# Reusing loaded weights in the state-space matmuls, joining the sample matmuls to the prompt matmuls, and claiming slots before the work

## The chip, the cores and the metric

One Trainium2 chip, all eight cores, two dies of four (cores 0 to 3 and 4 to 7). Each core runs the same program on its own prompt row and 16 sample rows. The metric is the device time in microseconds of the slowest core. Time before: 3663.6 us, median of 3 runs (3660.78 to 3669.47).

Some executions fall into a slow state, in which one die, sometimes both, has a lower granted TensorE clock and the run takes longer: 12 of the 39 executions of the kernel before in the rounds of the experiments took 3763.6 to 4310.9 us, with 0.81 to 0.95 on the slower die. Only fast runs (3657.7 to 3670.2 us for this kernel, clock 0.98 on all cores) are compared here. In the profile lines PE is TensorE, the matmul engine, and PEld its weight loads; DVE is VectorE, ACT ScalarE, POOL GpSimd and SP SyncE; L669 is line 669 of the kernel. Because the slowest of eight cores is a noisy number, I also give the *mean core*: the mean span of all cores of those dies whose mean granted clock was over 0.98, over all timed runs of the rounds named. For the kernel before it is 3654.6 us (80 cores, standard deviation 4.8 us).

## The reference, cut to what matters

Four layers. Each has a large input projection, a gated convolution, a state-space branch, a merge, an output projection and a feed-forward part. The change is in the state-space branch:

```python
bu = einsum('blgc,gpc->blgp', u, bbar)             # gather: input into the 64 complex states of each group
h  = associative_scan(a, bu)                       # state_t = Abar * state_{t-1} + Bbar u_t
y  = einsum('blgp,gcp->blgc', h, c) + d * u        # read the state out
ys = gelu(y); ys = ys * sigmoid(ys @ w_glu + b)
```

A prompt of 2048 positions is processed in two halves of 1024. The 16 sample rows, one step each, ride along with the first half.

## The kernel before: the parts that the change touches

The Python program records operations; a list scheduler with assumed costs then fixes one static order for each engine and assigns buffer slots. A tile takes its slot when the first operation that names it is scheduled. An operation is scheduled only if all its slots are there:

```python
def feasible(o, t):
    need = {}
    for tl in o.tiles:
        if tl.slot is None:
            need.setdefault(tl.pool, []).append(tl)
    for p, tls in need.items():
        if len(p.free) < len(tls):
            return False
        ...                                    # and a reserve for the tiles that come first in the program
```

One state-space pass (`ssm_f`, 4 a layer and half, so 32 in all) as PE sees it, cut. Every `e.matmul` makes two instructions, a weight load and a matmul (23912 of each on the page). The tilings are those that the kernel asks for and the profile prints: "array tiled 128x64" stands for matmuls with weights of 128 rows by 64 columns, placed at column 0 or 64 (two column groups; `128*64` at L1033), "64x128" for weights of 64 rows, placed at row 0 or 64 (two row groups; `64*128` at L1107), "full array" for weights of 128 by 128 (`128*128`):

```python
# gather: 32 matmuls of 64 columns, array tiled 128x64
gg[...]  += Wv(h)[:, q, g2, ri, :] . uv(h)[:, q, g2, :]          # S.pe(subs, [(gg,)], (128, 64))
if hs:                                                            # first half: 16 sample matmuls of 16 columns
    gsb[...] = Wv(0)[:, q, g2, ri, :] . us()[:, q, g2, :]         # its own S.pe, its own weight loads
...                                                               # DVE: rotate, scan, rotate back -> vt
# direct part of the output: 8 matmuls of 128 and 8 of 64 columns, full array
yb[g2] += KTv(0)[:, q, g2, :] . uvb()[:, :, q, g2, :]
yb[g2] += KTv(1)[:, q, g2, :] . uv(0)[:, q, g2, :]
if hs:                                                            # 24 sample matmuls of 16 columns, own S.pe
    ysb += KTv(0)[:, q, g2, :] . us()[:, q, g2, :]
    ysb += CDv(0)[:, q, ri, :] . AS0Z[:, g2, ri, 4 * f + q, :]    # ri = 0, 1
# state part of the output: 64 matmuls of 64 columns, array tiled 64x128, row groups g2 in turn
for q, h:
    for i, (o, ri, kk) in enumerate(((0, 0, 0), (256, 1, 0), (512, 1, 1), (768, 0, 1))):
        for g2 in range(2):
            yb[g2] += CDv(h)[64*g2:64*g2+64, q, ri, :] . vt[64*g2:64*g2+64, o+q*64:...]
```

The scheduler makes PE wait for its last operation where the tiling of the array changes (`o.forced = lastpe`).

## Time and profile before

| | before |
|---|---|
| median | 3663.6 us |
| PE busy | 96% |
| weight loads, matmuls | 23912, 23912 |
| start to start, projection matmul of 512 / 384 / 272 columns | 216 / 162 / 116 ns |
| start to start beyond the columns' own time, whole core | 237 us |

These lines are from the page of the kernel before: busy time, granted clock in 40 slices, the queue that brings instructions (packets, MB, share), the chain that ended last by engine, and the costliest groups (count, then busy us and mean ns, then idle time ahead of them).

```profile
span 3663.7 us, 67385 instructions; the slowest of 8 cores (3647.5 to 3663.7 us)
PE 3504.0 (96%) x23912; PEld 1979.7 (54%) x23912; DVE 1618.6 (44%) x2889; ACT 1141.7 (31%) x2151; POOL 608.7 (17%) x799
...
PEclk9799999999999999999999999999999999999999
...
q8 instruction: 202, 3.31, 0.4%
...
PE 88%; DVE 4%; issue 3%; DMA 3%; ACT 1%; SPq 1%; DVEq 0%; ACTq 0%; POOL 0%; POOLq 0%
...
L669 PE MATMUL ps<-H,RING 128*128 128x512 bf16 (+2 forms) x12160 | 2194.9, 340 | 23.5 <-DVE H L726 9.7
L669 PEld LDWEIGHTS ps<-H,RING 128*128 128x128 bf16 x12160 | 1191.5, 99 | 965.9 <-issue 52.3
```

PE is the bottleneck, and its projection matmuls (starts 216, 162 or 116 ns apart) hide their 99 ns loads. What a new order can win is 237 us in which PE stands still. The columns' own time in that figure is an estimate; at 216 ns for 512 columns the trace gives 238 us again (excesses of over 10 ns, slowest core).

### The profile page before, as it was taken

Reading aid. Unit: us, or ns where it says so; the run is one execution under the profiler, and the core shown is the slowest. Engines: PE = TensorE matmul, PEld = TensorE weight load, DVE = VectorE, ACT = ScalarE, POOL = GpSimd, SP = SyncE. Lnnn points to the kernel's source line nnn. Section 1 sums busy time; section 2 is a strip of 40 time slices with the busy share of each in tenths; the row PEclk is TensorE's granted clock in tenths of the full one; section 3 lists DMA queues with packets and bytes.
Section 4 is the critical chain, followed back from the end, with each engine's and each line's share of the span. In section 5 each row is a group of like instructions: output and inputs, shape, how many; then the busy total and the mean of one; then the engine's idle time right before and its main releaser. Section 6 shows DMA issues by size and latency. Waiting matters only on the chain.

```text
span 3663.7 us, 67385 instructions; the slowest of 8 cores (3647.5 to 3663.7 us)
## 1 busy us (share of the span) xinstructions
PE 3504.0 (96%) x23912; PEld 1979.7 (54%) x23912; DVE 1618.6 (44%) x2889; ACT 1141.7 (31%) x2151; POOL 608.7 (17%) x799
## 2 busy tenths in 40 slices
PE   6699999999999999999999899999999999999998
PEld 3466666666666666666664344444444444444443
DVE  8745555465454654543244331354224442254313
ACT  4443234332353322533134320243103421042202
POOL 4232210322103221030000200002000110002000
PEclk9799999999999999999999999999999999999999
DMA  7444557435574355854338544574445644474443
GB/s 157 115 82 70 114 139 149 87 66 113 138 155 86 62 113 135 185 110 84 70 71 196 116 77 71 98 169 74 75 77 115 144 70 81 70 146 79 79 72 87
DMA packets 252804, 384.14 MB, mean 105 GB/s; under 512 B 157632, under 2 KB 180800, under 8 KB 246848
## 3 DMA queue, kind: packets, MB, share of 16 engines
q0 software_dynamic: 67968, 243.30, 39.5%
q1 hardware_dynamic: 184512, 136.53, 12.8%
q8 instruction: 202, 3.31, 0.4%
q14 instruction: 122, 1.00, 0.1%
HBM read 567.06 MB, written 56.12 MB: 170 GB/s over the span
## 4 chain that ended last, share of the span: by engine, by line
PE 88%; DVE 4%; issue 3%; DMA 3%; ACT 1%; SPq 1%; DVEq 0%; ACTq 0%; POOL 0%; POOLq 0%
PE ps L669 83%; DMA yT<-X 1%; PE ps L702 1%; PE ps L1107 1%; DVE SC L561 1%; DVE H L726 1%; PE ps L1033 1%; PE ps L908 1%; PE ps L1080 0%; DVE X L1246 0%; DMA scv<-CIN 0%; SPq L632 0%; PE ps L895 0%; DMA X<-xsT 0%; DVE R L1225 0%
## 5 line engine op out<-in xcount | busy, mean ns | idle before, releaser
L669 PE MATMUL ps<-H,RING 128*128 128x512 bf16 (+2 forms) x12160 | 2194.9, 340 | 23.5 <-DVE H L726 9.7
L669 PEld LDWEIGHTS ps<-H,RING 128*128 128x128 bf16 x12160 | 1191.5, 99 | 965.9 <-issue 52.3
L669 PE MATMUL ps<-R,RING 128*128 128x384 bf16 (+2 forms) x6400 | 1162.1, 339 | 19.7 <-DMA R<-dy 11.4
L669 PEld LDWEIGHTS ps<-R,RING 128*128 128x128 bf16 x6400 | 624.2, 98 | 517.8 <-issue 35.4
L656 POOL DMA_DIRECT2D RING<-wpk x472 | 253.0, 537 | 2635.0 <-PE ps L669 2431.7
L1268 DVE TENSOR_TENSOR R<-SC,ps 128x384 bf16<-128x384 f32 (+2 forms) x440 | 255.8, 583 | 786.7 <-PE ps L669 773.6
L1267 ACT ACTIVATE SC<-ps 128x384 f32<-128x384 f32 (+2 forms) x440 | 226.1, 515 | 1208.0 <-PE ps L669 1199.6
L1246 DVE TENSOR_TENSOR X<-X,ps 128x384 f32<-128x384 f32 (+2 forms) x480 | 269.8, 582 | 448.2 <-PE ps L669 445.2
L700 ACT ACTIVATE H<-X 128x384 bf16<-128x384 f32 (+2 forms) x304 | 156.6, 539 | 198.4 <-DVE X L1246 178.7
L726 DVE SCALAR_TENSOR_TENSOR H<-X,PRM,SC 128x384 bf16<-128x384 f32 (+2 forms) x304 | 183.0, 672 | 35.0 <-ACT SC L707 34.8
L1240 POOL TENSOR_TENSOR R<-TB,SC 128x384 bf16<-128x384 f32 (+1 forms) x160 | 168.1, 1063 | 113.1 <-DVE SC L1237 101.4
L1237 DVE TENSOR_TENSOR SC<-SC,ps 128x384 f32<-128x384 f32 (+1 forms) x160 | 92.7, 584 | 163.5 <-PE ps L669 78.6
L1236 ACT ACTIVATE SC<-ps 128x384 f32<-128x384 f32 (+1 forms) x160 | 81.4, 515 | 248.2 <-PE ps L669 219.8
L1213 DVE TENSOR_TENSOR TB<-TB,ps 128x384 f32<-128x384 f32 (+2 forms) x160 | 89.9, 582 | 128.6 <-PE ps L669 124.6
L1172 DVE TENSOR_TENSOR CIN<-ps,SC 128x384 f32<-128x384 f32 (+2 forms) x80 | 47.0, 587 | 200.7 <-ACT SC L1171 192.6
L561 DVE TENSOR_TENSOR SC<-TB 128x512 f32<-128x512 f32 (+1 forms) x160 | 124.1, 785 | 8.1 <-PE ps L908 0.6
L1158 ACT ACTIVATE TB<-ps 128x384 f32<-128x384 f32 (+1 forms) x160 | 78.9, 516 | 85.8 <-PE ps L669 85.4
L702 PE MATMUL ps<-H,ONESB 128*128 128x384 bf16 (+2 forms) x320 | 78.1, 348 | 27.5 <-ACT H L700 26.8
L561 POOL TENSOR_TENSOR TB<-TB 128x512 f32<-128x512 f32 (+1 forms) x72 | 89.3, 1242 | 42.3 <-DVE R L835 20.7
L1225 DVE TENSOR_TENSOR R<-R,SC 128x384 bf16<-128x384 bf16 (+2 forms) x80 | 46.4, 588 | 88.8 <-ACT SC L1223 86.7
L899 ACT ACTIVATE TAB<-ps 128x512 bf16<-128x512 f32 x60 | 35.5, 597 | 133.0 <-PE ps L895 132.8
L1171 ACT ACTIVATE SC<-ps 128x384 f32<-128x384 f32 (+2 forms) x80 | 41.0, 513 | 95.7 <-PE ps L669 95.5
(180 smaller groups left out, 1633.1 us busy)
## 6 DMA issues: line engine op xcount, KB each, us to landing
RING<-wpk POOLq DMA_DIRECT2D x440, 512.0 KB, 7.0
TAB<-stash SPq DMA_DIRECT2D x21, 1792.0 KB, 10.0
stash<-TAB SPq DMA_DIRECT2D x15, 1792.0 KB, 7.6
R<-stash SPq DMA_DIRECT2D x7, 1792.0 KB, 14.8
RING<-wpk POOLq DMA_DIRECT2D x32, 384.0 KB, 6.1
du<-R SPq DMA_DIRECT2D x32, 256.0 KB, 9.2
UU<-du SPq DMA_DIRECT2D x32, 256.0 KB, 7.2
dy<-YY SPq DMA_DIRECT2D x32, 256.0 KB, 6.6
```

What stands on the lines that cost most here:

```text
L561: fn = lambda e: e.tensor_tensor(out=out(), in0=a(), in1=b(), op=op)
L656: S.dma("pool", lambda e: e.dma_start(out=t[:, 0:n], in_=wpk[l, ui, :, 0:n]), [("X",) + gate] if gate else (), [(t,)], 128 * n * 4, prio=- ...
L669: subs.append((lambda e, u=u, kw=kw, c=c, src=src, i=i: e.matmul(ps[:, 0:blk.n], lhsT=u.ap(kw, c), rhs=src(blk), start=(i == 0), stop=(i = ...
L700: act(lambda e, kt=kt: e.activation(out=hq(kt), in_=xin(kt)[0], func=AF.Square), xin(kt)[1], qkeys(kt, blk), n)
L702: S.pe([(lambda e, kt=kt: e.matmul(ps[:, 0:n], lhsT=ONESB[:], rhs=hq(kt), start=(kt == 0), stop=(kt == 7)), qkeys(kt, blk) + [C_("ONESB")] ...
L726: dve(lambda e, kt=kt, xi=xi, g=g: e.scalar_tensor_tensor(out=H[:, kt, blk.c0:blk.c0 + n], in0=xi(), scalar=g, in1=rs[:, 0:n], op0=ALU.mul ...
L1213: dve(lambda e, po=po, n=n, t_=t_, blk=blk: e.tensor_tensor(out=t_[:, blk.c0:blk.c0 + n], in0=t_[:, blk.c0:blk.c0 + n], in1=po[:, 0:n], op ...
L1237: dve(lambda e, sg=sg, po=po, n=n: e.tensor_tensor(out=sg[:, 0:n], in0=sg[:, 0:n], in1=po[:, 0:n], op=ALU.mult), [(sg,), (po,)], [(sg,)], n)
L1240: S.op(MENG, lambda e, sg=sg, n=n, t_=t_, blk=blk, j=j: e.tensor_tensor(out=R[:, MT[j], blk.c0:blk.c0 + n], in0=t_[:, blk.c0:blk.c0 + n], ...
L1246: dve(lambda e: e.tensor_tensor(out=X[:, j, blk.c0:blk.c0 + n], in0=X[:, j, blk.c0:blk.c0 + n], in1=ps[:, 0:n], op=ALU.add), [(ps,)] + xke ...
L1267: act(lambda e, sg=sg, pg=pg, n=n: e.activation(out=sg[:, 0:n], in_=pg[:, 0:n], func=AF.Silu), [(pg,)], [(sg,)], n, tset="silu")
L1268: dve(lambda e, sg=sg, pu=pu, n=n, blk=blk, ti=ti: e.tensor_tensor(out=R[:, ti, blk.c0:blk.c0 + n], in0=sg[:, 0:n], in1=pu[:, 0:n], op=ALU ...
```

## The change

Its intent: drop weight loads where the weights are already in the array (64 a pass in the first half, 32 in the second, 1536 of 23912), by placing matmuls on the same weights one after the other; join the sample matmuls to the prompt operations for that; and let an operation claim the slot of the tile that will be written later, so that the scheduler does not tie itself up. The core of the diff, with cuts:

```diff
+    def keep(e, out, lhsT, rhs, start, stop, tile=(128, 128), pos=(0, 0), skip=False):
+        return e.add_instruction(mybir.InstMatmult(
+            start_tensor_calc=start, stop_tensor_calc=stop, tile_size=tile, tile_position=pos, ldweights=False, ...))
-    def proj(parts, blk):
+    def proj(parts, blk, own=()):
...
-                [u.key] + keys(blk), MMN(blk.n)))
+                [u.key] + keys(blk) + list(own), MMN(blk.n)))
...                                            # table preparation: claim the table's slot
-                tt(zz1, lambda: Bv(me, 0), lambda o8=o8: Pv(pw, o8), ALU.mult, bkk, [(z1,)], 512)
+                tt(zz1, lambda: Bv(me, 0), lambda o8=o8: Pv(pw, o8), ALU.mult, bkk + [(tab, "own")], [(z1,)], 512)
...                                            # gather: sample matmul behind the prompt matmul, one operation
-            S.pe(subs, [(gg,)], (128, 64))
-            if hs:
-                ...
-                S.pe(subs, [(gsb,)], (128, 64))
+                            if hs and h == 0:
+                                subs.append((lambda e, ...: keep(e, gsb[...], Wv(0)[:, q, g2, ri, :], us()[:, q, g2, :], ...)))
+            S.pe(subs, [(gg,)] + ([(gsb,)] if hs else []), (128, 64))
...                                            # direct outputs: the same with ysb; CDv(0) loaded once for g2 = 0, 1
+            S.pe(subs, [(yb[0],), (yb[1],)] + ([(ysb,)] if hs else []), FULL)
...                                            # state outputs: two matmuls on one row group, one load
-                    for i, (o, ri, kk) in enumerate(((0, 0, 0), (256, 1, 0), (512, 1, 1), (768, 0, 1))):
+                    for ri, oo in ((0, (0, 768)), (1, (256, 512))):
                         for g2 in range(2):
-                            subs.append((... e.matmul(...), MMN(64) * 0.6))
+                            subs.append((... e.matmul(... vq(oo[0], q, g2) ...), MMN(64) * 0.5))
+                            subs.append((... keep(... vq(oo[1], q, g2) ...), MMN(64) * 0.5))
...                                            # gate projections claim the gate tile
-                    pg = projh(uga[jj // 2], jj % 2, blk)
+                    pg = projh(uga[jj // 2], jj % 2, blk, [(t_, "own")])
```

## The prediction

> **What bounds the kernel now.** TensorE. The page gives PE busy 96% of 3663.7 us; the chain of work that ended last is 88% PE, 83% on the projection line (L669). By the starts of successive matmuls a 128x512 projection matmul takes 216 ns, a 128x384 one 162 ns, a 128x272 one 116 ns, each with its own 98 ns weight load: the loads are hidden. Start-to-start time beyond that of the columns sums to about 237 us of PE standing still, 79 us of it in the first 200 us (table preparation on DVE; in the windows 50-100 and 100-150 us PE is busy 0.74 and 0.48), most of the rest at the eight layer starts. That is all a new order can win.
>
> **What the change touches.** L1033, L1043, L1080, L1083, L1093, L1097 and L1107: start to start 138 us in total, some 86 us of it dense issue. It removes 64 weight loads in each of 16 passes of the first half and 32 in each of 16 of the second (1536 of 23912); no matmul goes.
>
> - Sample matmuls of the gather (16 a pass): 0.23 to 0.25 us, 15.7 ns each, the pace of the 64-column ones, so weight loads set it. Reuse saves an estimated 0.1 us a pass.
> - Sample output matmuls (24 a pass): 25 ns each. Without 16 loads, an estimated 0.2 us a pass. Together about 5 us.
> - Each change of the array's tiling drains PE: 0.33 to 0.53 us start to start, 183 times, 99 us in all. In about 5 of 16 passes the gather and its sample part were issued apart; joining them saves about 3 us.
> - Output matmuls (64 a pass, both halves): 0.92 us, starts alternating 10 and 19 ns, two row groups side by side, 29 ns a pair against 27 ns of streaming. The loads are already hidden, so dropping half wins almost nothing, and two matmuls in a row on one row group may break the side by side order. [...] I expect 0.9 to 1.3 us a pass, 0 to 10 us lost.
>
> Net: about 3 us gained, 0.1%.
>
> **What moves.** The joined operations need three PSUM banks at once and wait for the later sample transfer in their middle (once now 4.9 us, near 597 us); the DVE scan behind them then waits too. Claiming the gate tile before its projections keeps PE from filling PSUM with results that cannot be drained (one such stall now: 5.5 us near 1970 us); claiming the table slot first delays a few DVE operations of the preparation. The static order of all engines is computed anew; I count this as a draw with a spread of some 25 us, slightly more to win than to lose.
>
> **Predicted: 3653 us, 3620 to 3690 8 times in 10. Faster by over 2%: 0.02; within 2%: 0.95; slower by over 2%: 0.03.**
>
> **What would show it.** Weight loads 22376, matmuls 23912. PE busy about 96%. Gather with samples about 0.6 us in one run (was 0.48 and 0.25); output matmuls not below 0.9 us a pass; about 170 tiling changes. L669 spacing unchanged. Idle in the first 200 us within 15 us of before.
>
> **What would make it wrong.** Output matmuls that fall to one row group at a time (27 ns each, 1.7 us a pass: 26 us lost); a new order of the preparation that moves the first 200 us by tens of us; PE going cold at layer starts (its granted clock fell to 0.59 in 100-150 us); three PSUM banks at once starving the projections.

5 us from the sample matmuls and 3 us from joining, less 0 to 10 us (5 in the middle) in the output matmuls, is the 3 us of the net. What is not measured in these terms is estimated: the 0.1 and 0.2 us a pass are my estimates beside the paces of 15.7 and 25 ns; that weight loads set the first pace was inferred, not shown; that the row groups' order may break was a fear that no trace had shown (the rulers below have pairs at 14.7 ns). The 27 ns for 64 columns is an estimate too, 216 ns x 64/512.

## More of the kernel before

The next fence is the timeline of PE in the second half (start, length, engine, line, operation, tiles, shape; in brackets the idle time ahead and what ended it). PE stops for 3.85 us in the middle of one operation, between two matmuls that wait for no semaphore:

```profile
2858.40 0.19 PE L1083 MATMUL ps<-UU,TAB 128*128 128x64 bf16 x1
2858.43 0.22 PE L1080 MATMUL ps<-UU,TAB 128*128 128x128 bf16 x1
2862.50 0.19 PE L1083 MATMUL ps<-UU,TAB 128*128 128x64 bf16 x1 [3.85 <-issue]
```

The "issue" entries are waits for nothing that the profile shows.

## The result, and the profile after

| | before | after |
|---|---|---|
| median | 3662.24 us (4 runs) | 3661.27 us (4 runs, one of them slow) |
| ratio of the fast runs | | 0.999 (0.9967 to 1.0012) |
| the same again, five rounds | | 0.9974 (0.9961 to 0.9987) |
| mean core | 3654.6 us | 3643.3 us |

A ratio is the mean time of one kernel's fast runs over that of the other's fast runs of the same rounds, so it is not quite the ratio of the quoted medians.

The time is the same within 2%, a small gain of 0.1 to 0.3%. The mean core, here that of the five rounds, gained 11.3 us (0.31%); the slowest of eight gained less, because the spans of the cores spread more (standard deviation 6.2 us, was 4.8). The 11.3 us are not sharp: the clock rule leaves out one die of a fast run of the change (clock 0.977; with it 3645.0 us), and the first four runs of the change give 3645.9 us (28 cores). A gain of about 9 to 11 us is what the runs support. The corresponding lines of the page after (the projection line is now L675):

```profile
span 3655.6 us, 65790 instructions; the slowest of 8 cores (3640.0 to 3655.6 us)
PE 3500.2 (96%) x23912; PEld 1976.1 (54%) x22376; DVE 1617.7 (44%) x2889; ACT 1136.3 (31%) x2146; POOL 610.6 (17%) x799
...
PEclk9899999999999999999999999999999999999999
...
q8 instruction: 196, 3.21, 0.4%
...
PE 87%; DVE 4%; issue 3%; DMA 3%; ACT 1%; SPq 1%; DVEq 0%; ACTq 0%; POOL 0%; POOLq 0%
...
L675 PE MATMUL ps<-H,RING 128*128 128x512 bf16 (+2 forms) x12160 | 2192.8, 340 | 23.7 <-DVE H L732 9.7
L675 PEld LDWEIGHTS ps<-H,RING 128*128 128x128 bf16 x12160 | 1190.0, 98 | 965.4 <-issue 52.4
```

1536 loads are gone and PE is as busy as ever; the other line that moved for a plain reason is the instruction queue, 196 blocks for 202.

**Where reuse did little or nothing.** First start to last start of one group of matmuls at full clock, the commonest value over all passes and cores:

| group | before | after |
|---|---|---|
| gather and samples, 48 matmuls, where they ran back to back | 0.76 us | 0.87 us |
| direct outputs and samples, 40 matmuls | 1.26 us | 1.26 us |
| state outputs, 64 matmuls | 0.92 us | 0.92 us |

The timeline shows why. Sample matmuls of 16 columns before (L1097 and L1093, each with a load; a merged row of x2 is two of them):

```profile
1063.55 0.17 PE L1093 MATMUL ps<-UU,TAB 128*128 128x16 bf16 x1
1063.57 0.19 PE L1097 MATMUL ps<-AS0Z,TAB 128*128 128x16 bf16 x2
1063.62 0.17 PE L1093 MATMUL ps<-UU,TAB 128*128 128x16 bf16 x1
1063.64 0.20 PE L1097 MATMUL ps<-AS0Z,TAB 128*128 128x16 bf16 x2
```

and after, where L1100 loads and L666 is the reuse:

```profile
1057.10 0.17 PE L1100 MATMUL ps<-AS0Z,TAB 128*128 128x16 bf16 x1
1057.12 0.17 PE L666 MATMUL ps<-AS0Z,TAB 128*128 128x16 bf16 x1
1057.15 0.17 PE L1100 MATMUL ps<-AS0Z,TAB 128*128 128x16 bf16 x1
1057.17 0.17 PE L666 MATMUL ps<-AS0Z,TAB 128*128 128x16 bf16 x1
```

Three starts in 0.07 to 0.08 us before, two in 0.05 us after: 25 ns each, load or no load.

The gather needs one more comparison, because the change did two things to it: it placed the sample matmuls between the prompt matmuls, and it dropped their loads. A version of the change with every weight loaded (below) keeps the order and takes the loads back. First and last start of one gather with samples there, on core 2:

```profile
1046.83 0.19 PE L1037 MATMUL ps<-UU,TAB 128*64 128x64 bf16 x1
...
1047.74 0.20 PE L1037 MATMUL ps<-UU,TAB 128*64 128x64 bf16 x1
```

and with reuse (the change again):

```profile
1046.02 0.19 PE L1039 MATMUL ps<-UU,TAB 128*64 128x64 bf16 x1
...
1046.88 0.20 PE L1039 MATMUL ps<-UU,TAB 128*64 128x64 bf16 x1
```

That is 0.91 us with the loads and 0.87 us without, the commonest values on all cores too. So the new order cost 0.15 us a gather (0.76 to 0.91), and reuse gave 0.04 us of it back.

**Where the time moved.** Taking the starts of the norm matmuls as marks, on the mean of eight cores of the two profiled executions, the feed-forward parts of all layers agree within 0.5 us. The differences are in the mixer parts: in the first half -4.1, +0.6, -3.4 and +2.6 us for the four layers, in the second half +1.0, -1.6, -4.1 and +0.1. So something other than the matmul pace saves a few microseconds here and there, and the experiments look for it.

### The profile page after: what moved, and what is told of

The parts are those of the page before. It is cut to its first block, busy times and chain, and to the rows that moved or that the text cites. A ratio compares the mean times of both kernels' runs of the same rounds, so it can differ in the third digit from the quotient of the medians.

```text
span 3655.6 us, 65790 instructions; the slowest of 8 cores (3640.0 to 3655.6 us)
## 1 busy us (share of the span) xinstructions
PE 3500.2 (96%) x23912; PEld 1976.1 (54%) x22376; DVE 1617.7 (44%) x2889; ACT 1136.3 (31%) x2146; POOL 610.6 (17%) x799
## 3 DMA queue, kind: packets, MB, share of 16 engines
q1 hardware_dynamic: 184512, 136.53, 12.9%
## 4 chain that ended last, share of the span: by engine, by line
PE 87%; DVE 4%; issue 3%; DMA 3%; ACT 1%; SPq 1%; DVEq 0%; ACTq 0%; POOL 0%; POOLq 0%
PE ps L675 83%; DMA yT<-X 1%; PE ps L708 1%; DVE SC L562 1%; DVE H L732 1%; PE ps L1039 1%; PE ps L666 1%; PE ps L1113 1%; DVE X L1255 0%; DMA scv<-CIN 0%; PE ps L914 0%; PE ps L1081 0%; SPq L633 0%; DMA dy<-YY 0%; DMA X<-xsT 0%
## 5 line engine op out<-in xcount | busy, mean ns | idle before, releaser
L675 PE MATMUL ps<-H,RING 128*128 128x512 bf16 (+2 forms) x12160 | 2192.8, 340 | 23.7 <-DVE H L732 9.7
L675 PEld LDWEIGHTS ps<-H,RING 128*128 128x128 bf16 x12160 | 1190.0, 98 | 965.4 <-issue 52.4
L675 PE MATMUL ps<-R,RING 128*128 128x384 bf16 (+2 forms) x6400 | 1162.8, 339 | 26.3 <-DMA R<-dy 16.4
L675 PEld LDWEIGHTS ps<-R,RING 128*128 128x128 bf16 x6400 | 624.2, 98 | 525.4 <-issue 43.5
L1276 ACT ACTIVATE SC<-ps 128x384 f32<-128x384 f32 (+2 forms) x440 | 226.1, 515 | 1208.1 <-PE ps L675 1204.4
L1198 ACT ACTIVATE SC<-CIN,PRM 128x384 f32<-128x384 f32 (+2 forms) x80 | 58.0, 726 | 32.5 <-DVE CIN L1181 32.4
```

Source lines behind the costliest of these rows:

```text
L675: subs.append((lambda e, u=u, kw=kw, c=c, src=src, i=i: e.matmul(ps[:, 0:blk.n], lhsT=u.ap(kw, c), rhs=src(blk), start=(i == 0), stop=(i = ...
L1276: act(lambda e, sg=sg, pg=pg, n=n: e.activation(out=sg[:, 0:n], in_=pg[:, 0:n], func=AF.Silu), [(pg,)], [(sg,)], n, tset="silu")
```

## The experiments

First theory: *nothing to reuse*, the loads were hidden and the 11 us come from the new static order. Rival: *reuse saves, the order gives it back*. Before any run, three versions of the change with one or both early claims taken out were tried: for each the scheduler ends with operations left over that wait for slots of each other. So both claims are needed for the joined operations to be scheduled at all.

In the table, "boundary stalls" is a sum per core, worked out from the trace: gaps over 0.5 us from start to start between two matmuls with no wait, ending 1.1 to 1.65 us after a block of PE's instructions has landed. The second condition hardly selects: in the kernel before, the change again and the change with all loads, all 125 gaps over 0.7 us with no wait ended 1.0 to 1.7 us after such a landing. "Half clock" is the time lost to a granted clock below full (the clock records of the slowest cores before and after hold 1.00 and 0.50 alone), mean of the cores, from the profiled run; for the change again it is die 0 alone (clock 0.987), because die 1 had a lower clock there (0.977; the profiled run of the result table lost 52 us on all eight cores). The stalls that some expectations name (13 us for the change, 27 us for the claims alone) are larger than the table's. The fast runs of a version are few: two for "empty in dense groups" and "all loads, shifted", three to five for the others. Every version also moves the block boundaries to other instructions, which turns out to matter.

| kernel | ratio of fast runs (95%) | fast runs, mean us | mean core, us | boundary stalls, us | half clock, us |
|---|---|---|---|---|---|
| before | 1 | 3662.4 | 3654.6 | 15.3 | 64 |
| change, again | 0.9974 (0.9961 to 0.9987) | 3655.5 | 3643.3 | 7.0 | 47 (die 0) |
| change, all loads | 1.0018 (1.0005 to 1.0031) | 3669.1 | 3660.2 | 19.1 | 60 |
| claims only | 0.9994 (0.9979 to 1.0009) | 3660.3 | 3647.5 | 17.9 | 58 |
| cost only | 1.0004 (0.9989 to 1.0019) | 3663.9 | 3656.2 | 17.1 | 62 |
| empty in dense groups | 1.0216 (1.0197 to 1.0236) | 3741.2 | not used | 1.7 | 78 |
| empty in projections | 0.9963 (0.9947 to 0.9979) | 3648.7 | 3639.8 | 5.8 | 51 |
| claims and output pairs | 0.9957 (0.9941 to 0.9973) | 3646.3 | 3637.4 | 9.7 | 49 |
| claims and summed pairs | 0.9929 (0.9915 to 0.9943) | 3636.0 | 3626.9 | 17.7 | 49 |
| all loads, shifted | 0.9970 (0.9944 to 0.9996) | 3653.0 | 3647.0 | 11.1 | 51 |
| change, summed pairs | 0.9904 (0.9883 to 0.9925) | 3629.2 | 3619.8 | 4.0 | 44 |
| change, shifted | 0.9985 (0.9961 to 1.0009) | 3658.9 | 3645.6 | 8.7 | 52 |

The mean core of before was 3653.8 to 3655.5 us in the other rounds. All outputs were correct.

### The change again

No edit.

> The changed kernel once more, in the same rounds as the next three. Both theories: 3655 to 3665 us, ratio to before 0.997 to 1.000; the median core of a run about 10 us (0.3%) shorter than that of before (3643 against 3655 us in the profiled runs), the slowest core less.

Measured: 0.9974, mean core 3643.3 us. The small gain is real: the interval excludes 1.

### The change with every weight loaded

```diff
     def keep(e, out, lhsT, rhs, start, stop, tile=(128, 128), pos=(0, 0), skip=False):
-        return e.add_instruction(mybir.InstMatmult(... ldweights=False ...))
+        return e.matmul(out, lhsT=lhsT, rhs=rhs, start=start, stop=stop, tile_position=pos, skip_group_check=skip)
```

> The changed kernel with its static order kept instruction by instruction, but every matmul loads its weights again (23912 loads instead of 22376). Theory 'nothing to reuse' (loads were hidden; a 16-column matmul starts 25 ns after the last one with or without a load): the same as the changed kernel to within 0.1% (4 us), group lengths equal: gather with samples 0.77 us, first outputs with samples 1.28 us, outputs 0.93 us. Rival 'reuse saves, the order gives it back': 5 to 10 us slower than the changed kernel, and sample groups longer by 0.1 to 0.2 us a pass.

Measured: mean core 3660.2 us, 17 us above the change; the direct and state outputs as in the change (1.26 and 0.92 us), the gather 0.91 us against 0.87. **Both theories missed.** The loads slow the gather by 0.04 us a pass (0.6 us over 16 passes) and the other groups not at all, so the first was nearly right on the pace; yet taking them away saves 17 us, where the rival allowed 5 to 10. The timeline of core 2 shows where; first with all loads, in the middle of the same operation as above:

```profile
1058.12 0.17 PE L666 MATMUL ps<-AS0Z,TAB 128*128 128x16 bf16 x1
1058.15 0.17 PE L1098 MATMUL ps<-AS0Z,TAB 128*128 128x16 bf16 x1
1060.73 0.18 PE L666 MATMUL ps<-AS0Z,TAB 128*128 128x16 bf16 x1 [2.41 <-issue]
1060.77 0.17 PE L1098 MATMUL ps<-AS0Z,TAB 128*128 128x16 bf16 x1
```

and the same place with reuse (the change again), which runs through into the next projection:

```profile
1057.53 0.17 PE L1100 MATMUL ps<-AS0Z,TAB 128*128 128x16 bf16 x1
1057.56 0.17 PE L666 MATMUL ps<-AS0Z,TAB 128*128 128x16 bf16 x1
1057.58 2.71 PE L675 MATMUL ps<-H,RING 128*128 128x384 bf16 x18
```

During the gap one packet of 16384 bytes of the instruction queue was on its way: it landed at 1059.43 us, and PE went on 1.30 us later. The stop near 2858 us of the kernel before is the same: block landed at 2861.07, PE on at 2862.50. In the kernel before the queue brings 202 packets, all of 16384 bytes, each under way for 0.89 to 1.99 us (median 0.96, slowest core). They are PE's blocks by their count: 23912 loads, 23912 matmuls and 3977 semaphore instructions are 256.4 for each of the 202, so 256 instructions in a block; in the kernel after (22376, 23912 and 3947; 196 packets) it is 256.3.

To see that it is the block boundary, I numbered PE's instructions in the three kernels where every matmul has a load (in the others the missing records cannot be counted). On the six cores whose traces are complete, 126 of the 127 boundary stalls of these kernels lie at 187 or 188 modulo 256 and one at 189 (cores 2 and 4 lack 166 records each, so their later numbers are off): before at number 9403, 17340, 25532, 42940; all loads at 9403, 17339, 17595, 25531, 37820, 42171, 42940; cost only at 9403, 17339, 25532, 42939. These are seen on core after core; a number can be off by one with the way of counting. The numbering also tells how far ahead the blocks come. On those cores, block transfer i (from 0) never began before PE was about 146 instructions past number 256 i, and PE stood still at 443 past it (443 is 187 modulo 256) if the block had not come: a lead of at most some 300 instructions.

A second effect follows a stall. Windows view of core 2 for the same 20 us (busy us and count for each engine, then granted clock, DMA share, GB/s), all loads first, then the change again:

```profile
1060.00:1080.00 20.00, 16.12 (x280) 11.80 (x281) 6.89 (x12) 9.40 (x21) 0.53 (x1) 0.83 0.52 113
```

```profile
1060.00:1080.00 20.00, 17.03 (x370) 12.58 (x241) 10.44 (x19) 12.55 (x27) 0.53 (x1) 1.00 0.78 164
```

With all loads the clock was halved for 3.4 and 6.8 us in this region after the stalls, on all eight cores; with reuse on none, in two profiled executions. That gave the second theory, *instruction supply*: in the dense groups PE uses up 256 instructions in an estimated 2 to 3 us (128 pairs of a load and a matmul, 15 to 25 ns a pair by the spacing above), faster than the next block comes; it stands still, then runs at half clock. Fewer instructions there, fewer stalls. Its rival: *the load itself* costs.

### The claims alone

```diff
 kernel before
-    ... bkk, [(z1,)], 512)                           +    ... bkk + [(tab, "own")], [(z1,)], 512)
-    pg = projh(uga[jj // 2], jj % 2, blk)            +    pg = projh(uga[jj // 2], jj % 2, blk, [(t_, "own")])
```

> The kernel before with the two early claims alone. If the claims made the 10 us on the median core: ratio 0.997 to 0.998 to before, first 200 us shorter. If they only let the joined operations be scheduled (without either claim the joined version finds no order at all): 0.999 to 1.001.

Measured: 0.9994 on the slowest core, not clear of 1; mean core 3647.5 us, 7.1 us less. The first layer's mixer is 10.8 us shorter, some of which is lost again in the third (+3.8). The windows view of the slowest core, before and then with the claims:

```profile
100.00:160.00 60.00, 33.65 (x496) 24.05 (x493) 44.24 (x68) 31.55 (x56) 13.00 (x12) 0.66 0.36 93
```

```profile
100.00:160.00 60.00, 47.89 (x589) 32.10 (x588) 54.27 (x90) 32.99 (x64) 13.52 (x13) 0.83 0.46 116
```

PE and DVE are both busier in this stretch and the clock falls less, as it would if the preparation is better packed. The claims are more than a key to the scheduler.

### Another static order of the kernel before

```diff
 kernel before
-   ... tkk + [(vt, 0), (vt, 1)], MMN(64) * 0.6))
+   ... tkk + [(vt, 0), (vt, 1)], MMN(64) * 0.5))
```

> The kernel before with one number of the scheduler changed (assumed cost of an output matmul 0.5 for 0.6), so another static order of the same instructions. Theory 'order lottery': moves by up to 10 us (0.3%) either way with no change in any group's length, which is as much as the whole change made. Rival: a net gain of the change beyond such a draw, then this one stays within 0.1% of before.

Measured: 1.0004, mean core 3656.2 us. This one draw moved little; a lottery of 10 us was not seen here, so the theory of a pure order lottery lost ground.

### Rulers

```diff
 kernel before, put into the second half, ahead of two feed-forward parts
+ for each of 16 patterns: 64 matmuls on constant tiles, results read by nobody
```

> The kernel before with sixteen blocks of 64 matmuls of constants put into two places of the second half where PE is warm (results discarded). Start to start, full array: 16 columns with a load each 25 ns; with a load at every second one, and with one load for all: theory 'nothing to reuse' says 25 ns too, rival 'loads set the pace' says about 17 and 10 ns. 64 columns: 28 ns with and without loads. Row tiles of 64 by 128, 64 columns: alternating groups with loads 14.6 ns, pairs on one group with one load 14.6 ns (as in the change), pairs with two loads 14.6 to 20 ns, two loads then two reuses 13.5 to 14.6 ns, one group only 27 to 28 ns. Column tiles, 16 columns: 15.7 ns with loads, 15.4 ns in reusing pairs by the first theory, below 12 by the rival.

Mean start to start at full clock:

| pattern of 64 matmuls | ns |
|---|---|
| full array, 16 columns: a load each / every second / one in all | 25.0 / 25.0 / 25.0 |
| full array, 4 columns, one load | 25.1 |
| full array, 64 columns: a load each / one in all | 29.1 / 29.2 |
| two row groups, 64 columns: in turn, a load each | 14.6 |
| two row groups: pairs, one load / two loads | 14.7 / 14.7 |
| two row groups: two loads, then two reuses | 14.6 |
| one row group only, a load each | 29.2 |
| two row groups, 16 columns: a load each / pairs with one load | 12.9 / 12.6 |

The scheduler moved nine of the sixteen patterns of the first place to the start of the program (8 to 39 us); those of them that ran before the first record of the granted clock are not counted.

On the full array and on row groups, a matmul costs its start slot and a load costs almost nothing beside it (0.3 ns at most), in every pattern that ran at full clock. The column-tiled patterns, which are the tiling of the gather, ran mostly at half clock and are not in the table. There, two column groups with 16 columns took 26.6 ns with a load each and 20.0 ns in pairs with one load, so at half clock the loads did slow them; at full clock only the version with loads was seen (15.7 ns). For the gather the evidence at full clock is therefore the kernel itself: 0.91 and 0.87 us. The rulers have less clock as well, a mean of 0.978 to 0.980 on their cores for 0.981 to 0.985 in the kernel before, where the two feed-forward parts behind the rulers lie in stretches at 1.00 (2416 to 2839 us and 2866 to 3269 us on the slowest core).

### The loads replaced by empty instructions, in place

```diff
 the change
     def keep(...):
+        e.nop()
         return e.add_instruction(mybir.InstMatmult(...))
```

> The changed kernel with each dropped weight load replaced by an instruction that does nothing, at the same place (1536). Theory 'instruction supply' (PE waits for its next 16 KB block of instructions, and then runs at half clock): as slow as with the loads, mean core 3655 to 3662 us, instruction stalls 22 to 30 us a core, stalls in the middle of gathers and outputs back near 1060 us and 2420 us. Rival 'the load itself costs': as fast as the changed kernel, mean core 3643 us, stalls 13 us. If the groups get longer at full clock (over 0.95 us for 64 outputs), the empty instruction has a cost of its own and this does not decide.

Measured: 1.0216, and the groups grew: 64 state outputs in 3.07 us (the commonest value) instead of 0.92, that is (3.07 - 0.92) / 32 = 67 ns for one empty instruction. As said beforehand, this does not decide. The stalls fell to 1.7 us, which fits blocks coming in time for a slower PE.

### The same number of empty instructions, in the projections

```diff
 the change, in proj(): 1536 projections get one empty instruction ahead of their fourth matmul
+        (e.nop() if pad and i == 3 else None, e.matmul)[1](
```

> The changed kernel with the same 1536 empty instructions, but one in the middle of a projection each, where a matmul takes 116 to 216 ns. 'Instruction supply' with the rate as its cause: near the changed kernel, 3643 to 3649 us a mean core, stalls 13 to 18 us, although as many blocks are fetched as with the loads (202). If only the number of instructions counted: 3655 to 3662 us.

Measured: 0.9963, mean core 3639.8 us, stalls 5.8 us. As many blocks are fetched as with all loads (202) and it is as fast as the change, rather 3.5 us faster. So the number of instructions alone does not cost the 17 us; their rate in the dense groups can. The rival is not excluded by this run, and the empty instructions also moved every block boundary, so the 3.5 us are not a reading of the rate.

### The stream shifted by half a block

```diff
 the change with every weight loaded
+            if e == "pe":
+                for _ in range(128):
+                    eng.nop()
             for o in self.order[e]:
```

> The changed order with every weight loaded (which stalls 19 us a core in the middle of operations, always where the running number of the PE instruction is 187 or 188 modulo 256: at 9403, 17339, 17595, 25531, 37820, 42171, 42940), with 128 empty instructions put ahead of PE's first, so that every operation lies half a block later in the stream. 'Instruction supply': stalls stay at 187 or 188 modulo 256 of the new numbering, so they happen at other matmuls (old numbers 59 or 60 modulo 256), and none at the old ones; their sum stays between 10 and 25 us. Rival 'something at those matmuls waits, a semaphore or a bank': they stay at the same matmuls, new residue 59 or 60. [...]

Measured: mean core 3647.0 us, 13.2 us *less* than without the 128 extra instructions; stalls 11.1 us (19.1). On all eight cores the stalls of the second to fourth layers moved to other matmuls, numbers 9659, 9915, 17084, 17339, 17851, 18108 and 25275 of the longer stream, again 187 or 188 modulo 256. None was at 59 or 60. The 128 empty instructions took 9.3 us in a row at the start; PE's first matmul came 1.8 us later than without them (10.7 us for 8.9). One of the stalls on core 2, in the middle of a gather (a 16 KB block landed between the two rows):

```profile
1070.12 0.20 PE L1040 MATMUL ps<-UU,TAB 128*64 128x64 bf16 x1
1072.43 0.28 PE L1040 MATMUL ps<-UU,TAB 128*64 128x64 bf16 x3 [2.12 <-issue]
```

The order of every instruction with a load or a matmul is the same in both kernels, and so are the loads. The stalls stay with the block boundary and not with the matmul. That excludes a semaphore or a bank as their cause, and *the load itself* as the cause of these 13 us. It also says that much of what reuse appeared to win may be where the boundaries fall.

### The change shifted by half a block

```diff
 the change
+            128 empty instructions ahead of PE's first, as above
```

> The changed kernel (reuse) with the same 128 empty instructions ahead of PE's first. With all weights loaded the half-block shift alone took the mean core from 3660.2 to 3647.0 us. If reuse helps at any alignment by using fewer instructions in the dense groups: mean core 3638 to 3645 us, stalls 4 to 9 us, at least 3 us below the shifted version with loads. If what looked like a gain of reuse was only a lucky alignment: 3645 to 3660 us, stalls 10 to 19 us.

Measured: mean core 3645.6 us, stalls 8.7 us; fast runs 3658.9 us against 3653.0 us of the shifted version with loads. At this alignment the two mean cores differ by 1.4 us, measured in different rounds and well within the spread of the cores (5 to 7 us), and on the slowest core the intervals of the two ratios overlap: no gain of reuse is shown here. At the other it won 17 us. The expectation of at least 3 us failed, and neither alternative holds alone: the stalls of reuse stay at 6 to 9 us at the three alignments tried (the change, its version with empty instructions in the projections, this one) against 11 and 19 us with loads, but its worth in time depends on the alignment.

### The claims and the output pairs, nothing joined

```diff
 claims only
+   state outputs in pairs with one load, as in the change; assumed cost left at 0.6, so the order is that of the claims alone
```

> The kernel before with the two claims and the reusing output pairs, nothing joined; its static order is that of the claims alone (3647.5 us a mean core, stalls 27 us). 'Instruction supply': 1024 instructions fewer in the densest groups, stalls 15 to 20 us, mean core 3635 to 3642 us, ratio to before 0.994 to 0.997, so better than both kernels. Rival 'reuse pays only with the joined samples': 3647 us as the claims alone.

Measured: 0.9957, mean core 3637.4 us, stalls 9.7 us (17.9 with the claims alone). Better than both kernels by the intervals against before. A third of the loads that the change drops stay and the sample joins are left out, so the joins are not needed for a gain of this size. The state outputs take 0.92 us here as well. Whether the 10 us over the claims alone would survive a shift was not run, so they are not shown to be the worth of reuse.

### The pairs summed first

```diff
 claims only
+   dve: vt[:, 0:512] += vt[:, 512:1024] with its halves swapped
-   for i, (o, ri, kk) in enumerate(((0, 0, 0), (256, 1, 0), (512, 1, 1), (768, 0, 1))):   # 64 matmuls a pass
+   for ri in range(2):                                                                     # 32 matmuls a pass
```

> The claims, and the two products of each output pair summed on DVE before the output matmuls, so 32 matmuls and 32 loads a pass instead of 64 and 64 (no reuse). Output group 0.47 us instead of 0.93 us, 32 times: 15 us less of PE; half the instructions in it. DVE adds 0.6 us a pass ahead of the outputs. 'Instruction supply' and 'a matmul costs its slot, not its load' together: mean core 3622 to 3635 us. If the added DVE step lies on the path at layer starts: 3640 to 3650 us. One more rounding to bf16 in the state output; expected still correct.

Measured: 0.9929, mean core 3626.9 us, 20.6 us less than the claims alone. The group takes 0.45 us instead of 0.92: 0.47 us in each of 32 passes is 15 us. The other 5 us or so are not explained; this version too has other block boundaries. The added DVE step is not seen in the time; it is an estimated 0.3 us a pass (9.3 us more of DVE for 32 more instructions, by the pages of the change with and without it, 1627.0 and 1617.7 us). The boundary stalls stayed at 17.7 us.

### The change with the pairs summed first

```diff
 the change
+   the same DVE sum, and 32 state output matmuls a pass, a load each
```

> The changed kernel, its output pairs summed on DVE first (32 matmuls and 32 loads a pass; no reuse left there), sample matmuls still reusing. The summed version without joining ran at 0.9929 of before (3637 us) with 17.7 us of instruction stalls left, most in the first half. If the reuse in the joined groups removes those: stalls 8 to 12 us, 3622 to 3634 us, ratio 0.989 to 0.992. If the order of the first layer costs what it did between the claims alone and the change (8 us): about as without joining, 0.991 to 0.994.

Measured: 0.9904 (0.9883 to 0.9925), fast runs 3626.1 to 3631.8 us, mean core 3619.8 us, stalls 4.0 us. It is the fastest version found, about 35 us below before, and correct (one more rounding to bf16 in the state output). It was run at one alignment only: the 15 us of the shorter group should hold at any, the fall of the stalls need not. The page of its slowest core (170 of its 22888 matmul records are missing from the trace):

```profile
span 3628.3 us, 64662 instructions; the slowest of 8 cores (3613.3 to 3628.3 us)
PE 3471.7 (96%) x22718; PEld 1958.5 (54%) x22376; DVE 1627.0 (45%) x2921; ACT 1143.3 (32%) x2152; POOL 608.3 (17%) x799
...
q8 instruction: 192, 3.15, 0.3%
```

## Why the prediction was right or wrong, point by point

The number was right: 3653 us (3620 to 3690) predicted, 3661.27 us measured, within 2%. Of the 10 us or so that the middle value lies below before, the mechanism gave 3; the rest was the guess of a lucky draw. The reasons were right in part.

- *PE is the bottleneck and loads are hidden in the projections; at most 237 us to win.* Right. L669 and L675 have the same spacing of 216, 162 and 116 ns.
- *Output matmuls: dropping loads wins almost nothing; 0.9 to 1.3 us a pass.* Right: 0.92 us, as before. The rulers show the same pace, 14.6 to 14.7 ns, in any order with any number of loads that was tried.
- *Weight loads set the pace of the sample matmuls; reuse saves 0.1 us and 0.2 us a pass, together about 5 us.* **Wrong.** This is the step that failed. The direct outputs with samples stayed at 1.26 us, the 25 ns being the start slot of a full-array matmul of 16 columns (25.0 ns with no loads at all). The gather with samples grew from 0.76 to 0.87 us, 16 times 0.11, so about 2 us lost: placing the sample matmuls between the prompt matmuls cost 0.15 us (0.91 us with every load), and dropping their loads won 0.04 us, not 0.1. So reuse was worth about 0.6 us in the pace of the groups, not 5. I had read a common pace of 16- and 64-column matmuls as the pace of their loads, and had not priced the new order.
- *Gather with samples about 0.6 us.* Wrong, 0.87 us.
- *Joining saves about 3 us of tiling changes; about 170 of them.* Wrong: 180 (183 before), and the claims alone, with nothing joined, have 180 too.
- *The sum of these, 3 us gained.* It came out near the truth by luck. At one alignment reuse won 17 us on the mean core with the order fixed; the stalls fell by 12 us with it (19.1 to 7.0), so most of this is instruction supply, which the prediction did not have.
- *The 4.9 us stop near 597 us is a wait for the sample transfer.* **Wrong.** On that core it lies at instruction 9403, a block boundary, and the corresponding stop in the second half, where there are no samples, should have warned me. The "issue" label was to be taken at its word: nothing that the profile shows.
- *Claims: delay a few operations of the preparation, free PSUM; a draw.* Partly wrong: alone they shorten the first layer by 10.8 us. In the whole change 4.1 us of that remain. And they are needed: without either, the joined operations find no order. The stop for the gate tile near 1970 us, which I had hoped they would remove, is still there (6.1 us from start to start in one matmul near 1962 us).
- *Idle in the first 200 us within 15 us of before.* Right: 79 us before, 74 us after, on the slowest cores.

Where the 11 us of the mean core came from is shown in its parts and not fully in its sum: the first layer (-4.1 us, claims), and fewer boundary stalls (-8.3 us, from 15.3 to 7.0), with less time lost to half clock after them. These overlap, so they are not added.

What stays open: how much reuse is worth at an average alignment (17 us at one, nothing shown at the other); why a block's transfer begins so late (near 2858 us it began 1.6 us after PE had stopped); whether the gains of the last three versions survive a shift; why the joined version keeps only 4 of the 10.8 us in the first layer.

## What to carry to other kernels

Price a small matmul by its start slot (25.0 ns here for 16 columns on the full array, with a load each or one in all), not by its weight load: removing matmuls paid (20.6 us for half of one group, 15 us of it in the pace of the group), removing loads changed the pace of one group of three, and that by 0.04 us. Where hundreds of tiny PE instructions run in a row, number the instructions at each unexplained "issue" gap and look at the number modulo 256 (187 or 188 at 126 of 127 stalls here), and compare its end with the landing of the instruction blocks (1.1 to 1.65 us earlier here). Before crediting a change of 0.3% with a mechanism, shift the instruction stream by half a block: here 128 empty instructions alone were worth 13 us.
